# A product of two 4096 x 4096 matrices with GELU: the order of ScalarE, VectorE and both transfer queues made anew

## The chip, the cores and the metric

The kernel runs on one core of a Trainium2 chip. Its engines are TensorE (PE, matrix products), VectorE (DVE), ScalarE (ACT), GpSimd (POOL) and SyncE (SP); the last two are used here for little else than to start transfers (DMAs). Each engine works off its own list of instructions in a fixed order and waits, at each one, for the events that it needs. The metric is the time of one execution on the device, in microseconds (us); lower is better. A change of about 0.3% is what a measurement of this kernel tells from none.

## The reference

```python
def reference(a, b):                      # a, b: 4096 x 4096, float32
    x = np.matmul(a, b)
    return 0.5 * x * (1 + np.tanh(np.sqrt(2 / np.pi) * (x + 0.044715 * x**3)))
```

## The kernel before

The product is computed in half precision by a scheme of Strassen's kind, at two levels: a block of the output is made of seven products (P1 to P7) of sums and differences of quarter blocks instead of eight products, and a quarter is partly cut so once more. After 35 products that only warm TensorE and 32 plain ones come 6640 matmuls of 128 x 128 by 128 x 512 or 256. Their operands are such sums: VectorE forms them (helper `combine2`, line 964: 128x2048 or 128x4096 halves), after it has turned the blocks of `a` (line 656, transposes of 32 x 32). VectorE also adds finished products into the output sums (lines 1322 and 1327, from the accumulators), ScalarE copies accumulators (line 1981 to 1984), applies the GELU (line 1296) and squares the inputs for a running check of their size (line 1408, with VectorE's additions of line 1413).

The inputs `in_a_dram` and `in_b_dram` come in by POOL's queue, in pieces of 128 KB (b) and 256 KB (a). Sums that are used again are stored to a scratch unit in memory (`k_unit`, 512 KB) by SP's queue and fetched again by POOL's. Results go out by SP's queue (`out_dram`). All tiles lie in cells of a fixed set, named bR_73 to bR_80, aT, aD, stage_86, stage_87 (big ones) and y (small ones); a load into a cell must wait until the last user of what was there is done.

**What sets the order.** The kernel's body first only records operations. Each of the helpers `pe`, `dve`, `act` and `dma` (lines 824 to 838) calls `plan.add` with an estimated duration and the cells read and written, and the operation gets the next number, 0 to 4687. A planner (class `Plan`, line 323) then does three things: `schedule` (line 404) plays the engines forward by those durations, and picks for each engine the ready operation that is due first; `moved_order` (line 493) takes the planned order of each engine other than PE and applies the table `AFTER` to it, pair by pair; `emit` (line 504) plays the durations through once more in that fixed order and issues all operations in the order of their planned starts. TensorE's own order is that of recording. The heart of `moved_order` is

```python
for n, m in AFTER:
    o, row = self.ops[n], order[self.ops[n].eng]
    row.remove(o)
    row.insert(row.index(self.ops[m]) + 1 if m is not None else 0, o)
```

so a pair (n, m) puts operation n directly behind operation m on its engine. The planner's idea of a transfer is in three tables of numbers: `MOVE` is how long one takes by itself (us), `WEIGHT` its share when others are under way, and `UNDER_WAY` says what is under way when the plan begins. At most eight transfers of a queue are outstanding (`LANES = 8`). On the chip none of these numbers exists; there only the order on each engine is left, and the waits that the cells demand.

Of the kernel before, what the change touches and what calls it, by code (L numbers as in the profile page):

```python
# [52 lines left out]
UNDER_WAY = {"POOL": [(0.68, 12.2)] * 4}  # L53
# [7 lines left out]
    "store": 1.345, "fetch": 1.38, "quarter": 1.6, "piece": 1.27, "out": 0.73, "raw_a": 1.3, "raw_b": 0.645,  # L61
    "raw_a0": 1.363, "raw_b0": 0.64, "tiny": 0.2, "out_half": 0.3,
}
WEIGHT = {
    "raw_a0": 1.31, "raw_b0": 1.06, "store": 2.0, "fetch": 2.42, "quarter": 2.16, "piece": 2.16, "raw_a": 1.11,
    "raw_b": 1.06, "out": 1.05,
# [15 lines left out]
def modes_of(**kw):  # L82
# [2441 lines left out]
```

## Time and profile before

| | |
|---|---|
| median of three runs | 1445.19 us (1443.98 to 1448.59) |
| profiled execution, whole time | 1448.0 us |
| its span (first to last instruction) | 1446.4 us |
| granted TensorE clock, mean | 0.999 |
| PE busy | 1419.4 us, 98%, 6707 matmuls |
| DVE busy | 1238.0 us, 86% |
| ACT busy | 692.1 us, 48% |
| POOL busy | 487.5 us, 34% |
| moved by transfers | 380.99 MB, 263 GB/s in the mean |

Busy time is the time in which an engine executes something. In a row of a timeline the first number is the start from the span's begin, the second the length, then engine, line of the kernel, operation, written and read tiles (buffer numbers left out), shape, and after x the count of like instructions that follow each other; in brackets the idle time ahead of the row and what ended it. In a row of the waits: the engine and the matmul's line, what it waited for, the time in all, how often, the longest. A row of the windows gives, for a stretch of time, its length, then the busy time and count of PE, of its weight loads, of DVE, ACT and POOL, then TensorE's clock, the share of the transfer engines in use, and GB/s. A row of DMA issues ends with the size of one and the median time from issue to landing.

### The profile page before, as it was taken

The numbers are of one execution on the slowest core, as the hardware profiler recorded it, in microseconds if no ns is written. First come the engines' busy times: TensorE is split into PE (matmuls) and PEld (weight loads), VectorE is DVE, ScalarE is ACT, GpSimd is POOL, SyncE is SP. The second block draws the span as 40 slices with busy tenths as digits, with TensorE's granted clock in tenths as the row PEclk, the third lists the DMA queues.
The fourth block names the chain that finished last, engine by engine and source line by source line (L and its number), as shares of the span: only waits on it lengthen the run. The fifth ranks groups of instructions, "written<-read, shape, count | busy, mean of one in ns | idle before, by whom it ended". The sixth has DMA issues, their size and how long they took to land. (4 is left out here: it accounts for less than half of the span.)

```text
span 1446.4 us, 19351 instructions
## 1 busy us (share of the span) xinstructions
PE 1419.4 (98%) x6707; PEld 656.3 (45%) x6707; DVE 1238.0 (86%) x1331; ACT 692.1 (48%) x1492; POOL 487.5 (34%) x892
## 2 busy tenths in 40 slices
PE   8989999999999999999999999999999999999998
PEld 3434455465444444444444444444444444444443
DVE  2997797998889999979897988887998998878876
ACT  4966656358866313543655313353463622333133
POOL 6554245054225152324423342332322231231220
PEclk9999999999999999999999999999999999999999
DMA  9999999999999998989979897998998967796773
GB/s 171 203 241 272 311 298 266 338 237 271 295 299 248 335 201 231 310 276 276 321 259 318 274 216 270 257 248 276 280 348 241 302 160 228 273 313 217 260 256 140
DMA packets 207674, 380.99 MB, mean 263 GB/s; under 512 B 20944, under 2 KB 119760, under 8 KB 207568
## 3 DMA queue, kind: packets, MB, share of 16 engines
q0 software_dynamic: 150400, 247.52, 71.7%
q1 hardware_dynamic: 57168, 132.15, 24.4%
q8 instruction: 55, 0.90, 0.2%
q14 instruction: 51, 0.42, 0.1%
HBM read 339.74 MB, written 134.22 MB: 328 GB/s over the span
## 5 line engine op out<-in xcount | busy, mean ns | idle before, releaser
L1972 PE MATMUL acc<-bR 128*128 128x512 f16 x1568 | 346.8, 379 | 0.4 <-DVE bR L964 0.2
L1972 PEld LDWEIGHTS <-bR 128*128 128x128 f16 x1984 | 193.9, 98 | 235.0 <-DVE bR L964 1.3
L1972 PE MATMUL acc<-bR,aT 128*128 128x512 f16 x1280 | 283.4, 379 | 4.8 <-DVE bR L964 3.9
L1972 PEld LDWEIGHTS <-aT 128*128 128x128 f16 x1664 | 162.6, 98 | 202.0 <-issue 6.2
L838 POOL DMA_DIRECT2D bR<-k_unit x224 | 121.4, 545 | 367.9 <-PE acc L1972 265.2
L964 DVE TENSOR_TENSOR bR<-bR 128x4096 f16<-128x4096 f16 (+1 forms) x114 | 210.6, 1858 | 29.6 <-PE acc L1972 20.3
L838 POOL DMA_DIRECT2D bR<-in_b_dram x320 | 173.6, 546 | 159.0 <-DMA bR<-in_b_dram 61.3
L1984 ACT COPY acc<-acc 128x512 f32<-128x512 f32 x168 | 95.7, 574 | 274.7 <-PE acc L1972 247.4
L1322 DVE TENSOR_TENSOR y<-acc,y 128x512 f32<-128x512 f32 x269 | 177.1, 685 | 25.1 <-PE acc L1972 24.2
L1972 PE MATMUL acc<-bR,aD 128*128 128x512 f16 x736 | 163.6, 379 | 0.0
L1296 ACT ACTIVATE y<-y 128x512 f32<-128x512 f32 x174 | 105.3, 625 | 112.2 <-DVE y L1322 111.9
L1972 PEld LDWEIGHTS <-aD 128*128 128x128 f16 x1024 | 100.2, 98 | 120.8
L744 PE MATMUL acc<-bR,aT 128*128 128x512 f16 x544 | 119.9, 379 | 2.2 <-DVE y L1322 1.2
L744 PEld LDWEIGHTS <-aT 128*128 128x128 f16 x768 | 75.1, 98 | 92.3 <-issue 3.3
L1981 ACT COPY y<-acc 128x512 f32<-128x512 f32 x114 | 66.4, 585 | 94.5 <-PE acc L1972 87.1
L1408 ACT ACTIVATE y<-bR 128x1024 bf16<-128x1024 f16 x83 | 84.9, 1051 | 36.5 <-DVE y L1413 33.8
L838 POOL DMA_DIRECT2D stage<-in_b_dram x104 | 56.3, 546 | 121.9 <-PE acc L1045 32.3
L744 PEld LDWEIGHTS <-aD 128*128 128x128 f16 x608 | 59.4, 98 | 77.9 <-DVE aD L964 4.2
L1972 PE MATMUL acc<-stage,bR 128*128 128x512 f16 x416 | 94.0, 379 | 0.0
L1413 DVE TENSOR_TENSOR y<-y 128x1024 bf16<-128x1024 bf16 x102 | 70.0, 688 | 25.6 <-ACT y L1408 24.0
L1972 PE MATMUL acc<-stage,aT 128*128 128x512 f16 x384 | 86.8, 379 | 0.0
L1327 DVE TENSOR_TENSOR acc<-acc,y 128x512 f32<-128x512 f32 x115 | 78.9, 693 | 5.3 <-ACT y L1981 5.0
(128 smaller groups left out, 1769.0 us busy)
## 6 DMA issues: line engine op xcount, KB each, us to landing
bR<-k_unit POOLq DMA_DIRECT2D x224, 512.0 KB, 7.8
out_dram<-y SPq DMA_DIRECT2D x194, 256.0 KB, 6.8
bR<-in_b_dram POOLq DMA_DIRECT2D x328, 128.0 KB, 7.0
k_unit<-bR SPq DMA_DIRECT2D x78, 512.0 KB, 7.0
stage<-k_unit POOLq DMA_DIRECT2D x60, 512.0 KB, 7.0
bR<-in_a_dram POOLq DMA_DIRECT2D x64, 256.0 KB, 9.2
k_unit<-stage SPq DMA_DIRECT2D x30, 512.0 KB, 8.0
out_dram<-bR SPq DMA_DIRECT2D x56, 256.0 KB, 6.7
```

The lines of the kernel that those rows point to most:

```text
L744: nc.tensor.matmul(acc, sa[:, j // 2, i * P : (i + 1) * P, j % 2], sb[:, j, :], start=start and j == 0, stop=stop and j == 3, skip_group_c ...
L838: return plan.add(queue, COST[queue], lambda: eng.dma_start(out=dst, in_=src), r=r, w=w, size=MOVE[what] * SPREAD, weight=weight, **kw)
L964: nc.vector.tensor_tensor(out=dst, in0=xa, in1=ya, op=ALU.add if op > 0 else ALU.subtract)
L1296: act("gelu", lambda: nc.scalar.activation(t, t, ACT.Gelu_apprx_tanh), [("f", f)], [("f", f)])
L1322: dve("add", lambda: nc.vector.tensor_tensor(out=sm(g), in0=bank(s, i), in1=sm(f), op=ALU.add), [("f", f)], [("f", g), ("p", s, i)])
L1327: dve("add", lambda: nc.vector.tensor_tensor(out=bank(s, i), in0=bank(s, i), in1=sm(f), op=ALU.add), [("f", f)], [("p", s, i)])
L1408: act("square", lambda t=t, src=src: nc.scalar.activation(t, src, ACT.Square), [c(cx)], [("f", f)], slack=60.0, lead=lead)
L1413: dve("add16", lambda t=t, u=u: nc.vector.tensor_tensor(out=u, in0=u, in1=t, op=ALU.add), [("f", f)], [("f", e)], slack=60.0, lead=lead)
L1972: nc.tensor.matmul(bank(w, i), sa[:, jx // 2, r * P : (r + 1) * P, jx % 2], bv[:, jx, :], start=p in "17" and jx == 0, stop=jx == NJ - 1, ...
L1981: act("copy", lambda: nc.scalar.copy(out=sm(f), in_=bank(w, i)), [("p", w, i)], [("f", f)])
L1984: act("copy", lambda: nc.scalar.copy(out=bank(*dst), in_=bank(*x)), [("p", *x)], [("p", *dst)])
```

## The change

The three tables of the planner's durations get other numbers, and `AFTER` is a new table of 1580 pairs instead of 1131. Nothing else is edited: both programs record the same 4688 operations with the same needs, the same tiles and the same cells, and TensorE's instructions stand in the same order. Of the 1286 operations recorded for VectorE 356 keep their place in the order, of ScalarE's 1150 it is 318, of POOL's 872 transfers 175, of SP's 397 transfers 127. Most moves are short: half of them pass by less than about 1.2 us of the engine's own work. The new table has more lines, so line numbers behind it are 63 higher in the changed kernel (964 is 1027, 838 is 901).

```diff
-UNDER_WAY = {"POOL": [(0.68, 12.2)] * 4}
+UNDER_WAY = {"POOL": [(0.68, 13.2)] * 4}
...
 MOVE = {
-    "store": 1.345, "fetch": 1.38, "quarter": 1.6, "piece": 1.27, "out": 0.73, "raw_a": 1.3, "raw_b": 0.645,
-    "raw_a0": 1.363, "raw_b0": 0.64, "tiny": 0.2, "out_half": 0.3,
+    "store": 1.31, "fetch": 1.291, "quarter": 1.6, "piece": 1.27, "out": 0.743, "raw_a": 1.304, "raw_b": 0.649,
+    "raw_a0": 1.377, "raw_b0": 0.6444, "tiny": 0.2, "out_half": 0.3,
 }
 WEIGHT = {
-    "raw_a0": 1.31, "raw_b0": 1.06, "store": 2.0, "fetch": 2.42, "quarter": 2.16, "piece": 2.16, "raw_a": 1.11,
-    "raw_b": 1.06, "out": 1.05,
+    "raw_a0": 1.263, "raw_b0": 1.13, "store": 2.06, "fetch": 2.18, "quarter": 2.16, "piece": 2.16, "raw_a": 1.22,
+    "raw_b": 0.98, "out": 1.14,
 }
...
 AFTER = [
...
-    (3139, 3166), (3161, 3146), (3156, 3161), (3515, 3370), (3516, 3386), (3520, 3516), (3599, 3579),
+    (3058, 3037), (3094, 3086), (3034, 3094), (3139, 3119), (3161, 3146), (3166, 3161), (3214, 3156),
...
 ]
```

What that does to the engines' lists is shown at three places. In each pair of lists the first is the kernel before, the second the changed one; a row is line, operation, tiles and shape, and x how many of the same follow each other.

The first place is VectorE's list in the stretch from about 84 to 93 us (rows 58 to 67 of its list before, 50 to 60 now). The matmuls that start at 94.38 need the second aD_84<-aD_81,aT_66 of the first list.

```order
L964 TENSOR_TENSOR aD_84<-aD_81,aT_66 128x2048
L964 TENSOR_TENSOR bR_74<-bR_76,bR_74 128x2048
L964 TENSOR_TENSOR bR_80<-bR_76,aD_82 128x2048 x2
L1322 TENSOR_TENSOR aD_83<-acc_105,aD_83 128x512
L964 TENSOR_TENSOR aT_72<-aT_66,aT_72 128x2048
L1322 TENSOR_TENSOR aD_83<-acc_106,aD_83 128x512
L1322 TENSOR_TENSOR y_89<-acc_108,y_89 128x512
L964 TENSOR_TENSOR aT_72<-aT_66,aT_72 128x2048
L1413 TENSOR_TENSOR y_96<-y_96,bR_78 128x1024
L964 TENSOR_TENSOR aD_84<-aD_81,aT_66 128x2048
```

```order
L1476 TENSOR_TENSOR y_97<-y_97,y_102 128x1024
L1027 TENSOR_TENSOR aT_72<-aT_66,aT_72 128x2048
L1476 TENSOR_TENSOR y_96<-y_96,bR_78 128x1024
L1027 TENSOR_TENSOR aD_84<-aD_81,aT_66 128x2048
L1476 TENSOR_TENSOR y_96<-y_96,bR_78 128x1024
L1385 TENSOR_TENSOR y_98<-acc_107,y_98 128x512
L1476 TENSOR_TENSOR y_96<-y_96,y_102 128x1024
L1027 TENSOR_TENSOR aD_82<-bR_74,bR_80 128x2048
L1385 TENSOR_TENSOR y_100<-acc_109,y_100 128x512
L1385 TENSOR_TENSOR y_99<-acc_108,y_99 128x512
L1027 TENSOR_TENSOR aD_82<-bR_74,bR_80 128x2048
```

The aD_84 operation needed at 94.38 stands as the fourth row of the second list, behind one of the two aT_72, ahead of both aD_82; the other aD_84 stands three rows further down, and one of the two bR_80 and the second aT_72 come later still.

The second place is POOL's list from about 127 to 165 us: loads of b, 128 KB each, into the cells bR_74, bR_76, bR_77 and bR_78, eight pieces to a cell, in the order in which the stage operations of VectorE use the cells. The last row of each list is the end of this run of loads.

```order
L838 DMA bR_74<-in_b_dram 32x4x512 x5
L838 DMA bR_76<-in_b_dram 32x4x512 x7
L838 DMA bR_77<-in_b_dram 32x4x512 x4
L838 DMA bR_78<-in_b_dram 32x4x512
L838 DMA bR_77<-in_b_dram 32x4x512
L838 DMA bR_78<-in_b_dram 32x4x512 x2
L838 DMA bR_77<-in_b_dram 32x4x512 x3
L838 DMA bR_78<-in_b_dram 32x4x512 x5
```

```order
L901 DMA bR_76<-in_b_dram 32x4x512 x3
L901 DMA bR_77<-in_b_dram 32x4x512 x3
L901 DMA bR_76<-in_b_dram 32x4x512 x2
L901 DMA bR_77<-in_b_dram 32x4x512 x2
L901 DMA bR_76<-in_b_dram 32x4x512
L901 DMA bR_77<-in_b_dram 32x4x512
L901 DMA bR_76<-in_b_dram 32x4x512
L901 DMA bR_78<-in_b_dram 32x4x512
L901 DMA bR_77<-in_b_dram 32x4x512
L901 DMA bR_78<-in_b_dram 32x4x512
L901 DMA bR_77<-in_b_dram 32x4x512
L901 DMA bR_78<-in_b_dram 32x4x512 x4
```

Before, all of bR_76 stands ahead of bR_77; now six loads of bR_77 stand between those of bR_76, and two of bR_78 further up still, among bR_74, where the second list does not reach. The last load of bR_76 stands eight entries later than before, and the last of the whole run is a load of bR_78 in both.

The third place is POOL's list from about 841 to 860 us, the loads of b into stage_86, bR_74, bR_77 and stage_87. The sum that VectorE forms from stage_87 is needed by the matmuls of 863.99.

```order
L838 DMA stage_86<-in_b_dram 32x4x512
L838 DMA bR_77<-in_b_dram 32x4x512 x5
L838 DMA bR_74<-in_b_dram 32x4x512 x3
L838 DMA stage_87<-in_b_dram 32x4x512 x8
L838 DMA bR_77<-in_b_dram 32x4x512
L838 DMA bR_75<-k_unit_233 128x2048
L838 DMA bR_78<-k_unit_254 128x2048 x2
```

```order
L901 DMA stage_86<-in_b_dram 32x4x512
L901 DMA bR_77<-in_b_dram 32x4x512 x3
L901 DMA stage_86<-in_b_dram 32x4x512
L901 DMA bR_74<-in_b_dram 32x4x512
L901 DMA bR_77<-in_b_dram 32x4x512 x2
L901 DMA bR_74<-in_b_dram 32x4x512 x3
L901 DMA stage_87<-in_b_dram 32x4x512 x8
L901 DMA bR_78<-k_unit_254 128x2048 x2
```

The one load of bR_77 that stood behind the eight of stage_87 stands ahead of them now, and the fetch into bR_75 behind the two of bR_78.

369 rows, old and new, of the table AFTER are left out of this document.

## The prediction
> **What bounds the kernel now.** I read the page first, then TensorE's waits, then TensorE's timeline, and at each stall the timeline of the engine that ended it.
>
> ```profile
> span 1446.4 us, 19351 instructions
> PE 1419.4 (98%) x6707; PEld 656.3 (45%) x6707; DVE 1238.0 (86%) x1331; ACT 692.1 (48%) x1492; POOL 487.5 (34%) x892
> DMA  9999999999999998989979897998998967796773
> PE acc L1972 40%; DMA bR<-k_unit 1%; DVE bR L964 1%; DMA stage<-in_b_dram 0%; POOL stage L838 0%; DMA bR<-in_b_dram 0%; POOL bR L838 0%; DVE stage L964 0%; DVE bR L1322 0%; DVE acc L1327 0%; ACT y L2150 0%; DVE y L1322 0%; DVEq L964 0%; POOLq L838 0%
> ```
>
> The reader is to see that TensorE has work for 98% of the span, that the transfers are full for the first 40% of it, and that the chain's last 40% are matmuls without a gap. TensorE's order is the same in both programs, so its work of 1419 us is a floor, and the change can move only the waits. Three of them lie in the first 55 us, where the first loads come in (line, releaser, us in total, times, longest):
>
> ```profile
> PE acc L2260 <- DMA bR<-in_b_dram: 4.5, 3, 2.9
> PE acc L773 <- DVE aT L656: 1.6, 1, 1.6
> PE acc L753 <- DVE table L811: 1.5, 1, 1.5
> ```
>
> No order cures these 7.6 us. The others, by TensorE's timeline (in brackets the wait ahead of the row):
>
> ```profile
> 94.38 3.63 PE L744 MATMUL acc<-bR,aD 128*128 128x512 f16 x16 [1.87 <-DVE aD L964]
> 99.06 7.07 PE L744 MATMUL acc<-bR,aT 128*128 128x512 f16 x32 [1.05 <-ACT acc L2384]
> 107.46 7.08 PE L744 MATMUL acc<-bR,aD 128*128 128x512 f16 x32 [1.33 <-DVE aD L964]
> 115.70 7.07 PE L744 MATMUL acc<-aD,aT 128*128 128x512 f16 x32 [1.17 <-DVE aD L964]
> 171.41 7.07 PE L744 MATMUL acc<-stage,aD 128*128 128x512 f16 x32 [0.29 <-DVE stage L964]
> 180.32 7.07 PE L744 MATMUL acc<-stage,aD 128*128 128x512 f16 x32 [1.85 <-DVE stage L964]
> 283.90 3.61 PE L744 MATMUL acc<-bR,aT 128*128 128x512 f16 x16 [1.20 <-DVE y L1322]
> 448.55 3.61 PE L1972 MATMUL acc<-bR,aT 128*128 128x512 f16 x16 [1.48 <-DVE bR L964]
> 622.35 3.40 PE L1972 MATMUL acc<-bR,aT 128*128 128x512 f16 x15 [0.75 <-DMA bR<-in_b_dram]
> 716.57 2.75 PE L1972 MATMUL acc<-bR,aT 128*128 128x512 f16 x12 [0.17 <-DMA bR<-k_unit]
> 863.99 7.08 PE L1972 MATMUL acc<-bR,aT 128*128 128x512 f16 x32 [2.38 <-DVE bR L964]
> ```
>
> They sum to 13.5 us, 0.9% of the span: the most that an order could cure.
>
> **94 to 116 us: VectorE's work, and one set of loads.** VectorE runs back to back here:
>
> ```profile
> 105.04 2.36 DVE L964 TENSOR_TENSOR aD<-aT,aD 128x2048 f16<-128x2048 f16 x2
> 113.29 2.36 DVE L964 TENSOR_TENSOR aD<-bR 128x2048 f16<-128x2048 f16 x2 [2.42 <-DMA bR<-in_b_dram]
> 75.00:120.00 45.00, 39.58 (x181) 17.61 (x181) 42.20 (x54) 25.31 (x79) 23.18 (x43) 1.00 1.19 247
> ```
>
> The new order puts the aD operation that released the matmuls of 94.38 well ahead, so most of that wait of 1.87 goes (an operation of the same matmuls moves down, to about its old place); and the copy on ScalarE behind the 1.05 starts earlier. The pair at 105.04 (first row), which releases 107.46, has the very same operations ahead of it in both orders. VectorE is busy 42.20 us of the 45 (the third engine in the last row), so that pair ends where it ended, at best 0.5 earlier: what the first two waits give is taken back by a longer wait at 107. The set of eight loads behind 113.29 comes two entries earlier in POOL's queue, each entry a 0.54 us issue: -1.1 us at 115.70. In sum TensorE gets to the next part 0.5 + 1.1 = 1.6 us earlier at most, and 0 at least.
>
> **157 to 187 us: a queue that keeps its length.** Between 120 and 185 us POOL issues one 128 KB load whenever one lands. VectorE's timeline shows two sets' last loads, and POOL's the spacing:
>
> ```profile
> 170.13 2.36 DVE L964 TENSOR_TENSOR stage<-bR,stage 128x2048 f16<-128x2048 f16 x2 [1.78 <-DMA bR<-in_b_dram]
> 179.04 1.23 DVE L964 TENSOR_TENSOR stage<-bR,stage 128x2048 f16<-128x2048 f16 x1 [1.80 <-DMA bR<-in_b_dram]
> 162.63 1.22 DVE L964 TENSOR_TENSOR stage<-bR,stage 128x2048 f16<-128x2048 f16 x1
> 147.11 0.54 POOL L838 DMA_DIRECT2D bR<-in_b_dram  x1 [0.81 <-DMA bR<-in_b_dram]
> 156.50 4.44 POOL L838 DMA_DIRECT2D bR<-in_b_dram  x7 [0.37 <-DMA bR<-in_b_dram]
> bR<-in_b_dram POOLq DMA_DIRECT2D x328, 128.0 KB, 7.0
> 120.00:185.00 65.00, 62.86 (x291) 28.37 (x290) 49.58 (x64) 45.16 (x59) 20.65 (x39) 1.00 1.12 306
> ```
>
> Three sets of eight stand in this queue: bR_76 (for the stage operation of 162.63), bR_77 (170.13) and bR_78 (179.04). Now bR_78 and bR_77 have loads ahead of the last of bR_76, whose issue moves from 147.11 back by eight entries, to the second of the seven of 156.50, 157.2. With 7.0 us to landing (page, median) it lands at 164.2, and the operation ends 1.22 later at 165.4. The matmuls that wait for it began at 164.05 (171.41 less the wait of 0.29 and the 7.07 of a group of 32): a new wait of 1.4 us, or 0 if loads come in faster. The late end: the load that ended the wait at 170.13 is the fifth of those seven; eight entries took 157.2 - 147.11 = 10.1 us, 1.3 each, so three entries ahead of it is 166.2, plus 1.22, a wait of 3.4. But the last entry of the queue is a load of bR_78 as before, behind the same bytes on transfers that are full (1.12 in the last column but one), so 179.04 and with it 180.32 stay. The new wait and the 1.6 us gained up to here both end in the wait of 1.85 there. Net of both parts: **0**. The bounds: if the queue's last landing comes 1.85 earlier, the waits of 0.29 and 1.85 and the 1.6 us all count, -3.7; if bR_76 lands at the late end, TensorE comes 3.4 - 0.29 - 1.85 = 1.3 too late, +1.3.
>
> Here the Trainium skill, DMA: Bandwidth & Descriptors, Two DMAs through the same engine are not ordered, says that transfers start in order in a queue and may finish in another. By that, the +0.5 at 863.99 below could be 0 and the time 1444.2. The trace does not agree for these sets: the loads that end the waits at 170.13 and 179.04 are those issued last of their eight, so I keep the places.
>
> **283.90.** VectorE shows no idle ahead of either of the first two rows below. One operation of the pair aD<-aT,aD (1.22 us) goes behind the released one, and in their place come two y additions from further up.
>
> ```profile
> 282.03 1.22 DVE L964 TENSOR_TENSOR aD<-aT,aD 128x2048 f16<-128x2048 f16 x1
> 283.16 2.48 DVE L1322 TENSOR_TENSOR y<-acc,y 128x512 f32<-128x512 f32 x4
> 446.21 2.29 DVE L964 TENSOR_TENSOR bR<-bR 128x4096 f16<-128x4096 f16 x1 [1.66 <-DMA bR<-in_a_dram]
> ```
>
> By work alone the wait of 1.20 goes; by those additions, which wait for ScalarE, nothing does. I take the middle, **-0.6** (-1.2 to 0.2).
>
> **448.55** hangs on the transfer ahead of 446.21 (last row above), and the last of its loads has the same entry of the queue: **0** (-0.5 to +1.3, the spacing of one entry, since the set ahead has its last load one entry later).
>
> **622.35 and 716.57** wait for a load each that stands one entry earlier now: -0.75 and -0.17, **-0.9** (0 at the other end).
>
> **863.99.** POOL issues the eight loads of stage_87 here, and VectorE's sum waits for the last:
>
> ```profile
> 850.41 4.87 POOL L838 DMA_DIRECT2D stage<-in_b_dram  x8 [0.65 <-DMA bR<-in_b_dram]
> 855.38 0.54 POOL L838 DMA_DIRECT2D bR<-in_b_dram  x1
> ```
>
> The one load of bR_77 that stood behind them (855.38, 0.54 us) goes ahead: **+0.5** (0 to 1.1).
>
> **All else**, 866 to 1440 above all, has no wait now, and can only get one. Some fifteen operations move later by 0.5 to 5 us against a margin of 0.2 to 2 us. I price one wait of 283.90's size (1.20) at a bit under half its odds: **+0.5** (0 to 4).
>
> **Sum**: 0 - 0.6 + 0 - 0.9 + 0.5 + 0.5 = -0.5. The profiled execution took 1448.0 us (span 1446.4, 1.6 around it), 2.8 over the median of the runs shown, 1445.19; that 2.8 is no part of the change. Forecast: 1448.0 - 0.5 = 1447.5 on the profile's footing, **1444.7** on the median's.
>
> **Rival 1, faster: the first half's transfers come earlier.** The order rests on corrected durations, and it starts SP's second store of bR_73 directly behind its first; POOL waits for that cell here:
>
> ```profile
> 95.27 3.55 POOL L838 DMA_DIRECT2D bR<-in_b_dram  x6 [2.67 <-DMA stage<-in_b_dram]
> ```
>
> If this gap of 2.67 closes and the whole queue up to 180 us moves up with it, the -3.7 above counts. With 283.90 (-1.2) and -0.9, less 0.5: -5.3, so **1439.9**. For it: the gap is there. Against it: the transfers are already at 1.19 in that window, so bytes that start earlier push others later. The Trainium skill, Trainium Kernel Development and Optimization, Key Constraints, says the same of all queues, that they share 16 engines and interleave; by it this rival gives nothing and 1444.7 stands. Stores that fall behind loads can still shift some time, so I leave it **0.27**.
>
> **Rival 2, slower: a store goes late and its fetch stops POOL.** One of SP's two stores k_unit<-stage of 861.66 moves nine entries down, behind the first out store of 886.30; its fetch stays at POOL's 885.38.
>
> ```profile
> 861.66 0.87 SPq L838 DMA_DIRECT2D k_unit<-stage  x2
> 886.30 5.57 SPq L838 DMA_DIRECT2D out_dram<-y  x3
> 885.38 1.16 POOL L838 DMA_DIRECT2D stage<-k_unit  x2
> 912.35 3.62 PE L1972 MATMUL acc<-stage,aD 128*128 128x512 f16 x16
> k_unit<-stage SPq DMA_DIRECT2D x30, 512.0 KB, 8.0
> stage<-k_unit POOLq DMA_DIRECT2D x60, 512.0 KB, 7.0
> ```
>
> Store at 886.7, landed 8.0 later at 894.7; fetch then, landed 7.0 later at 901.7 (both medians): TensorE needs it at 912.35, so 10.6 us are left, and POOL is held from 885.4 to 894.7, 9.3 us. It decides once the held fetches, 512 KB each, queue up to more than those 10.6. Were half of the 9.3 to reach TensorE, with like ones for some later stores, it is +5.2 with the rest of my sum: **1450.4**. For it: nothing before 1440 us recovers a wait after 866, TensorE being without a gap. Against it: the margin is longer than the hold. **0.20**, with the other new waits in the unpriced rows.
>
> **How the numbers follow.** A change of 0.3% (4.3 us) is about what a measurement can tell from none: the three runs lie that far apart. My forecast, no measurable difference, has **0.53**, rival 1 **0.27**, rival 2 **0.20**. Its own range is 1441.5 to 1448.5 (below, the -3.7 against one more late wait of 0.5; above, the two bounds of 1.3 and one more wait of 1.2). To leave out two in ten I go to **1438.5** (rival 1 with the 1.48 of 448.55 too) and **1451** (just past rival 2). Faster 0.27, same 0.53, slower 0.20.
>
> **What would show it.** Right: in the new profile 180.32 stays within 1 us, a wait at about 164 is new, the waits at 94 and 99 are gone and that at 107 is longer; 622 and 717 have none; 864 has one of about 2.9. Rival 1 is shown by a set bR_78 that is complete before 177 us; rival 2 by TensorE waiting for stage<-k_unit after 900. I am wrong if waits after 866 sum to more than 4 us, or if the matmuls of 180.32 start over 3 us earlier.

## The result: 0.7% slower

The changed kernel takes 1455.60 us in the median of five runs (1452.75 to 1461.24), the kernel before 1444.87 us beside it (1443.98 to 1448.59): a ratio of 1.0072, 95% interval 1.0052 to 1.0092. The forecast was 1444.7 us with a range up to 1451; the result lies above it. The profiled execution of the changed kernel took 1452.75 us, the fastest of its five, and that of the kernel before 1448.0, near its slowest. So the two traces differ by 4.8 us and the medians by 10.7 us, and part of the work below is to say which differences between the traces are of the change.

The page of the changed kernel, its span, busy times and the chain that ended last:

```profile
span 1451.2 us, 19253 instructions
PE 1422.7 (98%) x6707; PEld 656.8 (45%) x6707; DVE 1235.9 (85%) x1331; ACT 685.2 (47%) x1492; POOL 487.8 (34%) x892
PE acc L2035 62%; PE acc L807 15%; DMA bR<-in_b_dram 5%; DMA stage<-in_a_dram 3%; DMA bR<-k_unit 3%; PE acc L1108 3%; DMA bR<-in_a_dram 2%; POOL bR L901 1%; DMA stage<-k_unit 1%; POOL stage L901 1%; DMA stage<-in_b_dram 1%; DVE stage L1027 1%; DVE bR L1027 0%; ACT y L1471 0%; DMA out_dram<-y 0%
```

TensorE has the same matmuls and 3.3 us more busy time. The half-rate clock told of below takes 3.9 us of it in the changed kernel and, at 23 us, 1.5 us in the kernel before. The 62% of the chain on matmuls lie in pieces with waits between them, the last at 1221.28, while the 40% before were one run of matmuls from 863.99 on: the late stalls have changed places. TensorE's timeline at the places that the prediction named, and at the new ones:

```profile
77.32 0.38 PE L807 MATMUL acc<-bR,aT 128*128 128x512 f16 x1 [1.67 <-DMA bR<-in_b_dram]
77.86 8.54 PE L807 MATMUL acc<-bR,aT 128*128 128x512 f16 x31 [0.16 <-DMA bR<-in_b_dram]
100.04 3.62 PE L807 MATMUL acc<-bR,aT 128*128 128x512 f16 x16
105.09 3.61 PE L807 MATMUL acc<-bR,aT 128*128 128x512 f16 x16 [1.43 <-ACT acc L2447]
109.78 7.08 PE L807 MATMUL acc<-bR,aD 128*128 128x512 f16 x32 [1.08 <-DVE aD L1027]
116.69 7.07 PE L807 MATMUL acc<-aD,aT 128*128 128x512 f16 x32
172.46 19.89 PE L807 MATMUL acc<-stage,aD 128*128 128x512 f16 x81 [7.26 <-DVE stage L1027]
290.75 3.62 PE L807 MATMUL acc<-bR,aT 128*128 128x512 f16 x16
455.31 3.61 PE L2035 MATMUL acc<-bR,aT 128*128 128x512 f16 x16 [1.02 <-DVE bR L1027]
867.01 7.07 PE L2035 MATMUL acc<-bR,aT 128*128 128x512 f16 x32
968.45 3.40 PE L2035 MATMUL acc<-bR,aD 128*128 128x512 f16 x15 [0.91 <-DMA bR<-in_b_dram]
1221.28 3.63 PE L2035 MATMUL acc<-bR 128*128 128x512 f16 x16 [0.31 <-DVE bR L1027]
```

Read each start against that of the same matmuls before. The lag is 100.04 - 99.06 = 1.0 us, at the next part of the program still 116.69 - 115.70 = 1.0; then 172.46 - 164.05 = 8.4; 290.75 - 283.90 = 6.9; 455.31 - 448.55 = 6.8; 867.01 - 863.99 = 3.0; and 4.8 at the end of the span. In this pair of traces one wait of 7.26 us, at the matmuls of the stage operand, is the largest loss, and the stall at 863.99, now gone, gives some 3 us back. The other 6 of the 10.7 us between the medians lie in executions that left no trace.

The wait of 7.26, by VectorE's timeline of the changed kernel:

```profile
169.44 1.23 DVE L1027 TENSOR_TENSOR stage<-bR,stage 128x2048 f16<-128x2048 f16 x1 [9.29 <-DMA bR<-in_b_dram]
171.19 1.22 DVE L1027 TENSOR_TENSOR stage<-bR,stage 128x2048 f16<-128x2048 f16 x1
```

It is the set bR_76 that comes late, as the prediction had it, but at 169.2 and not at 164.2: its last load, the row below, was issued at 158.54 (forecast 157.2) and took 10.6 us to land (forecast 7.0).

```profile
158.54 0.54 POOL L901 DMA_DIRECT2D bR<-in_b_dram  x1 [0.96 <-DMA bR<-in_b_dram]
```

Behind the landing stand three operations and not one. VectorE forms the stage operand in two halves, and each needs the whole set bR_76. The half that TensorE's first matmuls need stands second in both lists, behind the other half and the additions between. In the kernel before it is the prediction's row at 162.63; the other half is this one:

```profile
159.07 1.22 DVE L964 TENSOR_TENSOR stage<-bR,stage 128x2048 f16<-128x2048 f16 x1
```

In the changed kernel the landing is at 169.17, the halves are formed at 169.44 and 171.19 with one addition between them, and TensorE starts at 172.46, 3.3 us behind the landing where the prediction had 1.22.

What lies beside the load is in SP's list. SP's timeline before, where the long gap ahead of 156.50 is a wait of the queue at one out store, and then after:

```profile
144.71 0.44 SPq L838 DMA_DIRECT2D k_unit<-stage  x1
156.50 0.33 SPq L838 DMA_DIRECT2D out_dram<-y  x1
156.88 0.93 SPq L838 DMA_DIRECT2D k_unit<-aD  x2
157.91 1.36 SPq L838 DMA_DIRECT2D k_unit<-stage  x1
```

```profile
144.21 0.33 SPq L901 DMA_DIRECT2D k_unit<-aD  x1
147.00 1.64 SPq L901 DMA_DIRECT2D k_unit<-stage  x2
157.72 2.26 SPq L901 DMA_DIRECT2D out_dram<-y  x2
```

One store of aD and one of a stage cell, 512 KB each, have moved from behind that out store to ahead of it. Between the issue and the landing of the last bR_76 load six stores land in the changed kernel, 2.25 MB. The moved store of the stage cell is one of them; that of aD is not, it lands at 156.4.

Last, the windows around both new stalls, after and then before (the clock is the last column but two):

```profile
75.00:85.00 10.00, 8.17 (x31) 3.16 (x29) 9.95 (x13) 6.95 (x12) 7.30 (x13) 0.83 1.23 185
165.00:175.00 10.00, 2.74 (x8) 0.87 (x7) 5.12 (x7) 5.42 (x7) 2.16 (x4) 0.76 1.05 245
175.00:185.00 10.00, 10.00 (x43) 4.32 (x42) 9.90 (x11) 4.72 (x6) 0.00 (x0) 0.90 0.77 301
```

```profile
75.00:85.00 10.00, 10.00 (x47) 4.60 (x47) 9.72 (x14) 9.69 (x22) 4.90 (x9) 1.00 1.32 199
165.00:175.00 10.00, 9.71 (x46) 4.32 (x45) 7.44 (x9) 3.38 (x4) 0.54 (x1) 1.00 1.12 308
```

Behind each of the two new waits the granted clock is below 1: for eight to ten matmuls TensorE starts one in 0.43 us instead of 0.216. It costs 1.7 us at 77 us and 2.25 at 172 us, and no sentence of the prediction had a price for it. The kernel before shows one, behind a wait of 2.88 us: 25 matmuls take 7.09 us there and not 5.56, which is 1.5 us.

```profile
23.20 7.09 PE L2260 MATMUL acc<-bR,aT 128*128 128x512 f16 x25 [2.88 <-DMA bR<-in_b_dram]
```

### The profile page after: what moved, and what is told of

It reads as the page before. It is cut to its first block, busy times and chain, and to the rows that moved or that the text cites. A ratio compares the mean times of both kernels' runs of the same rounds, so it can differ in the third digit from the quotient of the medians.

```text
span 1451.2 us, 19253 instructions
## 1 busy us (share of the span) xinstructions
PE 1422.7 (98%) x6707; PEld 656.8 (45%) x6707; DVE 1235.9 (85%) x1331; ACT 685.2 (47%) x1492; POOL 487.8 (34%) x892
## 4 chain that ended last, share of the span: by engine, by line
PE 79%; DMA 14%; POOL 2%; DVE 2%; issue 2%; ACT 1%; DVEq 0%; POOLq 0%; ACTq 0%
PE acc L2035 62%; PE acc L807 15%; DMA bR<-in_b_dram 5%; DMA stage<-in_a_dram 3%; DMA bR<-k_unit 3%; PE acc L1108 3%; DMA bR<-in_a_dram 2%; POOL bR L901 1%; DMA stage<-k_unit 1%; POOL stage L901 1%; DMA stage<-in_b_dram 1%; DVE stage L1027 1%; DVE bR L1027 0%; ACT y L1471 0%; DMA out_dram<-y 0%
## 5 line engine op out<-in xcount | busy, mean ns | idle before, releaser
L2035 PE MATMUL acc<-bR,aD 128*128 128x512 f16 x736 | 163.8, 379 | 0.9 <-DMA bR<-in_b_dram 0.9
L807 PEld LDWEIGHTS <-aD 128*128 128x128 f16 x608 | 59.8, 99 | 82.3 <-issue 10.6
```

What stands on the lines that cost most here:

```text
L807: nc.tensor.matmul(acc, sa[:, j // 2, i * P : (i + 1) * P, j % 2], sb[:, j, :], start=start and j == 0, stop=stop and j == 3, skip_group_c ...
L2035: nc.tensor.matmul(bank(w, i), sa[:, jx // 2, r * P : (r + 1) * P, jx % 2], bv[:, jx, :], start=p in "17" and jx == 0, stop=jx == NJ - 1, ...
```

## The experiments

All of them give an engine a list that is put together from the kernel before and the changed kernel; no work differs. In the diffs `b` is the order before and `c` the changed one, of the four engines VectorE, ScalarE, POOL and SP. A cut at a time stands for the nearest place of the program at which both orders have issued the same entries: at 120 us these are the first 103, 145, 111 and 12 entries of the four engines, at 188 us 164, 207, 148 and 51. The kernel gets each list by a table `AFTER` that is made anew for it. Some of these kernels hold the old planner's numbers and some the changed; the list of each engine is the one told either way. Ratios are to the kernel before, run beside it.

**Which half.** The first two kernels cut the program at 188 us.

```diff
-order = c
+order = b[:188 us] + c[188 us:]      # e1_early_before
+order = c[:188 us] + b[188 us:]      # e2_late_before
```

> All four engines in the order of the kernel before up to about 188 us, in the changed order from there on. In the changed kernel TensorE is 8.2 us behind the kernel before at 188 us and 5.0 behind at the end. Theory A (the changed order is better behind 188 us: it removed the waits at 284, 622 and 864): those 3.2 us come without the early loss, 1444.9 - 3.2 = about 1441.7. Theory B (TensorE only came later, and so found done what it had waited for; the order behind 188 us gives nothing): the old waits are back and only the new ones at 964, 1213 and 1216 (1.1 + 0.5 + 0.5) are added, about 1445 to 1447.

> The other half: changed order up to about 188 us, order of before from there on. Theory A: the early loss of 8.2 us stays and nothing is won back, 1444.9 + 8.2 = about 1453. Theory B: the lateness is won back at the old waits (1.2 + 1.5 + 0.75 + 2.4 = 5.8 at most), 1444.9 + 8.2 - 5 = about 1448.

With the changed order late: 1.0015 (0.9998 to 1.0032). With the changed order early: 1.0097 (1.0080 to 1.0115), with the same wait. That is 12 us by the medians, more than the 8.2 that either theory started from. TensorE's timeline of e2:

```profile
170.30 21.89 PE L753 MATMUL acc<-stage,aD 128*128 128x512 f16 x89 [6.92 <-DVE stage L973]
870.61 8.75 PE L1981 MATMUL acc<-bR,aT 128*128 128x512 f16 x32 [3.11 <-DVE bR L973]
```

The loss is made in the first 188 us. All that the trace shows as gained behind that is not to be seen in the medians: of the late part alone no gain is measured, and its interval leaves room for 0.02% at most.

**The first 80 us, and the loads of 120 to 170 us.** In the second of these, POOL's entries 111 to 147 (37 loads) stand as before.

```diff
 order = c
+order = b[:80 us] + c[80 us:]                                  # e3_first80_before
+order["POOL"] = c[:111] + b[111:148] + c[148:]                 # e4_pool_loads_before
```

> The changed order, but with the order of before on all four engines up to about 80 us, where the changed kernel has new waits (1.7 us at 77 and a slower clock for 1.7 us behind it). Theory C (the loads of 120 to 170 us decide, in the order in which they stand): the wait at 172 stays within 2 us of 7.3, total within 2 us of the changed kernel, 1453.6 to 1455.6. Theory D (these loads are late because all of the queue starts 2.3 us later at 88 us): the wait at 172 shrinks by 2.3 or more and the total by 3 or more, 1452.5 or less.

> The changed order, but POOL's 37 loads of about 120 to 170 us in the order of before; all else as changed. Theory C: the wait of 7.3 us at 172 goes but for 1 to 2 us, and with it the slower clock behind it (2.1 us); TensorE is 1 to 3 us behind the kernel before at 188 us instead of 8.2, total 1447 to 1450. Theory D: the set of loads still comes late, the wait stays above 4 us, total above 1452.

e3: 1.0091 (1.0064 to 1.0118), no gain. The mixture makes a wait of its own, and the old one stays, by TensorE's timeline of e3:

```profile
122.01 8.61 PE L807 MATMUL acc<-aD,aT 128*128 128x512 f16 x32 [6.98 <-DVE aD L1027]
177.61 14.55 PE L807 MATMUL acc<-stage,aD 128*128 128x512 f16 x54 [5.55 <-DVE stage L1027]
```

So e3 says nothing of the first 80 us by itself, beyond that the wait at the stage operand doesn't need them. e4: 1.0037 (1.0023 to 1.0050); the wait at 164 to 172 is gone, and one of 2.42 stands at 174.20 in its place. The order of those loads is needed for the wait of 7 us. The whole time lies 5.8 us above the kernel before, more than the 2 to 5 us of theory C.

**The loads alone, and pieces of the late part.**

```diff
 order = b
+order["POOL"] = b[:111] + c[111:148] + b[148:]                 # e6_only_pool_loads
+order = b[:188 us] + c[188:905 us] + b[905 us:]                # e5_middle_after
+order = b[:736 us] + c[736:905 us] + b[905 us:]                # e8_736_to_905
```

> The kernel before with one thing of the change: POOL's 37 loads of about 120 to 170 us in the changed order. If that order makes the wait at 172 by itself (theory C): a wait of 4 to 8 us where TensorE starts on the stage operand of bR_76, a slower clock for 2 us behind it, 5 to 8 us slower in all (0.35 to 0.55%). If it needs the later start of the queue or the other engines' new order too: under 3 us.

> Order of before up to about 188 us and again from about 905 us on, the changed order only between. In the profiled run of the kernel with the changed order all the way behind 188 us, TensorE gained 5.2 us on the kernel before between 188 and 865 us and lost 1.5 behind (waits at 964 and 1216). Theory A (the changed order is better between): 3 to 5 us faster than before, 0.2 to 0.35%, and at 864 no wait. Theory B (that profiled run was a lucky one; its ten times had the median of the kernel before): within 1 us of before.

> The kernel before with the changed order only between about 736 and 905 us. The forecast had +0.5 us at 864 here, the changed kernel showed -2.6. If the order of this stretch takes the wait at 864 away by itself (POOL's fetches ahead of the loads leave its eight places earlier): no wait at 864, a new one of 0.5 at 788, 2 to 3 us faster. If the wait went for what came before 736 us: the wait of 2.4 us stays, no change.

e6: 1.0030 (1.0011 to 1.0050), and a wait inside the bounds that the prediction gave this term (1.4, at most 3.4). TensorE's timeline of e6, then VectorE's:

```profile
166.06 22.43 PE L745 MATMUL acc<-stage,aD 128*128 128x512 f16 x96 [2.93 <-DVE stage L965]
```

```profile
161.23 1.23 DVE L965 TENSOR_TENSOR stage<-bR,stage 128x2048 f16<-128x2048 f16 x1 [4.11 <-issue]
164.79 1.22 DVE L965 TENSOR_TENSOR stage<-bR,stage 128x2048 f16<-128x2048 f16 x1
```

The last bR_76 load is issued at 154.69 and lands 6.3 us later, at 161.0; one store, 0.25 MB, lands in that time. That is 3.2 us sooner than the forecast landing of 164.2, and the wait is still twice the 1.4: VectorE's old list has three additions between the two halves, and 5.1 us go from the landing to TensorE's start. So the number lay inside its bounds by luck, by two errors that cancel. From e6 to the changed kernel the landing is 8.2 us later, VectorE is 1.8 us shorter behind it, and TensorE itself comes 2.1 us later; that makes the 4.3 us between the two waits. e5 gives 1.0003 (0.9990 to 1.0016), so the waits that vanish between 188 and 905 us in the trace show no gain in the median. e8 gives 0.9983 (0.9968 to 0.9998), the only kernel of this study below 1: 1445.02 us in the median. That is below the 0.3% that a measurement tells from none, and the lowest of fifteen kernels. The wait at 864 is gone in it, by POOL's timeline and then TensorE's:

```profile
847.04 4.80 POOL L847 DMA_DIRECT2D stage<-in_b_dram  x8 [0.42 <-PE acc L1981]
```

```profile
860.24 7.07 PE L1981 MATMUL acc<-bR,aT 128*128 128x512 f16 x32
```

POOL issues the eight loads of stage_87 here 860.24 - 847.04 = 13.2 us ahead of the matmuls that need their sum. Before, it was 863.99 - 850.41 = 13.6 us with the wait of 2.38 in it, so 11.2 without. They come 2 us earlier in the program, and that is the wait. It is not the place of the one bR_77 load behind them, on which I had put the price: 0.54 us can't make 2.

**What makes the landing 8 us later.** I took first POOL's stop ahead of two early loads of bR_78, then SP's list.

```diff
 order = c
+order["POOL"]: the two early loads of bR_78 behind the last of bR_76    # e7_two_loads_back
+order["SP"] = b[:51] + c[51:]                                          # e9_stores_before
+order["SP"] = b[:51] + c[51:]; order["POOL"] = c[:111] + b[111:148] + c[148:]   # e12_both_before
```

> The changed kernel with two loads of bR_78 (the first of that set, ahead of the last loads of bR_74) put behind the last load of bR_76. Two things follow: POOL no longer stops at 133 to 137.6 us for the cell of bR_78, which ScalarE frees (4.35 us of waiting there), and the last load of bR_76 stands two entries earlier (1.3 us each). Theory E (the stop at the head of the queue counts): the wait of 7.3 us at 172 shrinks by 4 to 5 us. Theory C alone (only the entries count): by 2.6 us. Total 3 to 6 us faster than the changed kernel.

> The changed kernel with SP's first 51 stores (up to about 188 us) in the order of before. Theory F (the wait of 7.3 us at 172 is the eight entries of POOL's queue plus about 1 MB of stores that SP now issues at 144 to 148 us instead of 157 us, so that they compete with the last loads of bR_76): the wait shrinks from 7 to about 3 us, as in the run with POOL's loads alone, and the wait of 1.8 us at 75 goes too (SP's second store of bR_73 is issued at 83 instead of 55 us); 5 to 8 us faster than the changed kernel, 1447 to 1451. Theory G (the loss comes from VectorE's and ScalarE's order and from the later start of the queue): the wait at 172 stays above 5.5 us.

> The changed kernel with both taken back: SP's first 51 stores and POOL's 37 loads of 120 to 170 us in the order of before. Theory F: no wait above 1.5 us between 160 and 185 us, TensorE there within 2 us of the kernel before, total within 0.2% of before (1443 to 1449). Theory G: more than 0.3% slower than before stays.

e7: 1.0045 (1.0028 to 1.0062), and the wait is 6.88 at 170.89, nearly the same: a miss. The last bR_76 load is issued 3.7 us earlier, at 154.79, and takes 13.0 us to land instead of 10.6, with 2.75 MB of stores beside it. So an earlier place in POOL's queue alone gains little there. e9: 1.0022 (1.0004 to 1.0040). With SP's stores as before, and the loads in the changed order, both new waits are gone, at 77 and at 172 us; the last bR_76 load is issued at 154.56 and lands 6.0 us later with 0.5 MB of stores beside it. What is left is a wait that this mixture makes, at 143 us, where ScalarE waits for a store of a cell that it will overwrite. It makes TensorE 4.2 us later; without it TensorE would have come to the stage operand about 2.9 us too early (an estimate: 165.1 less 4.2, against 163.8, when VectorE has formed the half that it needs). So the landing is what e9 shows, 8.6 us sooner, and not that the whole wait goes with the stores. ScalarE's timeline of e9, then TensorE's:

```profile
141.51 1.06 ACT L1471 ACTIVATE y<-stage 128x1024 bf16<-128x1024 f16 x1 [7.45 <-DMA out_dram<-y]
```

```profile
143.59 1.02 PE L807 MATMUL acc<-bR,aT 128*128 128x512 f16 x4 [3.25 <-ACT acc L1575]
```

e12 gives 1.0027 (1.0009 to 1.0044), with no wait between 160 and 185 us and one of 4.66 at 145.42 of the same kind. So SP's order is what the late landing needs beside the loads' order. It does not say how much of the order before can be kept without a new wait.

**One store, and loads with stores, put into the kernel before.**

```diff
 order = b
+order["SP"] = c[:4] + b[4:]                                            # e10_one_store_early
+order["POOL"] = b[:111] + c[111:148] + b[148:]; order["SP"] = b[:13] + c[13:51] + b[51:]   # e11_loads_and_stores
```

> The kernel before with one store moved: SP's store of bR_73's second half first instead of fourth, so at about 55 instead of 83.6 us. If it is this 0.5 MB that makes the loads of 60 to 75 us late: a wait of about 1.8 us at 75 us and a slower clock behind it, TensorE 2 to 4 us later at 80 us; of which most is taken back by shorter waits up to 116 us. If not, TensorE is where it is before at 80 us, within 0.5 us. Total within 2 us of before in both cases.

> The kernel before with POOL's 37 loads of about 120 to 170 us and SP's stores 14 to 51 (about 121 to 188 us) in the changed order, nothing else. POOL's loads alone gave a wait of 2.9 us at 166. Theory F: with the stores it is 6 to 8 us, with 2 us of slower clock behind it, 6 to 9 us slower than before in all. Theory G: 2 to 4 us as with the loads alone.

e10: 1.0000 (0.9983 to 1.0016). The store of 54 us gives a wait of 1.19 at 75.70, where runs with the order before up to there have 0.41 at most, and no half-rate clock; the median doesn't show it. So the store alone is not the price of the first 80 us. e11: 1.0043 (1.0027 to 1.0058); the last bR_76 load is issued at 155.59 and lands 9.3 us later, at 164.9, with 2.0 MB of stores beside it: between the 161.0 of the loads alone and the 169.2 of the changed kernel. TensorE itself was late there by a wait of 3.15 at 117.98, again one of the mixture, so its own wait was only 1.83, less than either theory had.

**Cut where nothing is mixed.** The last three kernels avoid such mixtures by cutting all four engines at 120 us.

```diff
 order = b
+order = b[:120 us] + c[120:188 us] + b[188 us:]                        # e13_120_to_188
+order = c[:120 us] + b[120 us:]                                        # e14_first_120
+order = c[:120 us] + b[120:736 us] + c[736:905 us] + b[905 us:]; order["SP"][:4] = b[:4]   # e15_best
```

> The kernel before, with the changed order on all four engines only between about 120 us and 188 us of the program; the order before stands ahead of that and behind it. If this stretch by itself makes the loss (SP's two stores to k_unit and POOL's loads both in it): a wait of TensorE of at least 5 us between 160 and 175 us, with the half-rate clock of about 2 us behind it, and 0.4 to 0.7% slower than before. If the loss needs what the changed first 120 us do to SP and POOL as well: a wait of about 3 us there, as with the 37 loads alone, and at most 0.35% slower.

> The kernel before, with the changed order on all four engines only up to about 120 us; the order before stands behind that. If the first 120 us hold the rest of the loss: the wait of 1.8 us at 75 us and 1.7 us of half-rate clock behind it, 0.2 to 0.4% slower than before. If the waits that go between 94 and 116 us take that back: within 0.15% of before, with TensorE's lag at 116 us near 1 us and no new wait between 160 and 175 us.

> A candidate: the changed order up to about 120 us, but SP's first four stores as before, then the order before up to 736 us, the changed order from 736 to 905 us, and the order before behind. If the waits at 94, 99 and 116 us (some 2 us net) and the one at 864 us (2.5 us) are both worth their length: 0.2 to 0.35% faster than before, and faster than the 736 to 905 us stretch alone (0.9983). If the early waits are made up for later on before's own order: no better than that stretch alone.

e13, the stretch alone: 1.0019 (1.0003 to 1.0036). e14, the first 120 us alone: 1.0040 (1.0021 to 1.0059). TensorE's timeline of e13 and then of e14:

```profile
165.85 20.88 PE L748 MATMUL acc<-stage,aD 128*128 128x512 f16 x96 [2.66 <-DVE stage L968]
```

```profile
76.41 0.38 PE L746 MATMUL acc<-bR,aT 128*128 128x512 f16 x1 [1.66 <-DMA bR<-in_b_dram]
76.98 8.54 PE L746 MATMUL acc<-bR,aT 128*128 128x512 f16 x31 [0.20 <-DMA bR<-in_b_dram]
866.41 8.43 PE L1974 MATMUL acc<-bR,aT 128*128 128x512 f16 x32 [3.76 <-DVE bR L966]
```

In e14's trace TensorE is 3.4 us behind the kernel before at 81 us, level with it at 118 us (0.1) and at 188 us (-0.1), and 3.8 us behind at the end; 2.7 of these arise at 866.41, where the order is that of before. So where the 0.40% of the first 120 us arise is not shown.

The stretch from 120 to 188 us, with the same loads and stores in the same order as in the changed kernel, waits 2.66 and not 7.26. The wait of 7 us needs both parts. The waits of SP's queue from 120 to 135 us show what the first part hands on, in the changed kernel and then in e13:

```profile
SPq L901 <- DMA stage<-in_b_dram: 5.1, 1, 5.1
```

```profile
SPq L842 <- DMA stage<-in_b_dram: 1.7, 1, 1.7
```

Ahead of the stores in question stands one, `k_unit<-stage`, that waits for the last load of a stage cell. That load lands at 129.5 in the changed kernel and at 124.5 in e13. Of the stores behind it eight go 5 to 6 us later, the store of aD at 144.21 where it went at 138.46 in e13; the store of a stage cell that was moved ahead lands at 159.7 where it landed at 153.6. In e13 these stores are through when the last bR_76 load is issued, at 156.41: 0.25 MB land beside it, and it takes 6.1 us. In the changed kernel the two stores of stage cells issued at 147 to 148 us stand beside it, with those behind them: 2.25 MB and 10.6 us. That fits e9 too, where the moved stores stay behind the out store and the load lands, at 160.6, before the first of them (162.6). This chain is read from the two traces; no run moves that one load of the stage cell alone. Of the 6.6 us from 162.6 (e13) to 169.2, 4.5 are the longer transfer and 2.1 the later issue. In numbers of the last landing: before 156.9; the 37 loads alone 161.0; loads and stores of the stretch 162.6; with the first 120 us 169.2.

By medians the two parts alone are worth 0.19% and 0.40%, 0.59% in sum, and both together 0.97% (e2): the rest, 0.38% or 5.5 us, is what they do to each other. The three intervals together leave about 0.3% either way, so this rest is only just clear of zero. The two waits differ by 4.6 us, and the half-rate clock of 2.25 stands behind the long one alone: 6.9 us, which agrees within that margin.

e15 gives 1.0001 (0.9988 to 1.0015), 1447.32 us: no better than e8. It has two waits at 141 to 144 us that neither kernel has (0.78 and 1.31, for ScalarE's copy), which take back most of the early gains; whether these would last without them stays open. No version here beats the kernel before by more than e8's 0.17%.

## Why the prediction was wrong, point by point

The step that failed is the term of 157 to 187 us, which the prediction put at 0: a late set bR_76 whose wait would vanish in the wait of 180.32. It cost 7.2 us between the two traces.

The terms of the sum, in us, against the change of TensorE's lag between the two profiled executions (starts of the same matmuls; a row takes in all that lies between the row above and its place):

| place | forecast | measured |
|---|---|---|
| up to 90 us | 0 (not spoken of) | +4.2 |
| 94 to 116 | -1.6 to 0 | -3.2 |
| 157 to 187 | 0 with the part above | +7.2 |
| 283.90 | -0.6 | -1.4 |
| 448.55 | 0 | -0.1 |
| 622.35 and 716.57 | -0.9 | -0.7 |
| 863.99 | +0.5 | -3.0 |
| all else | +0.5 | +2.0 |
| sum | -0.5 | +5.0 |

**157 to 187 us is the term that decided it.** That bR_76 would come late, and that a wait of the stage matmuls would be new, was right. The size, 1.4 with an end at 3.4, was counted from places in POOL's queue alone. From start to start the wait is 7.4 us. Of the 6.0 beyond the forecast, the landing gives 5.0 (1.3 by the later issue, 3.6 by the longer transfer) and the other half of the stage operand and the addition, which VectorE does first, 2.1; TensorE itself came 1.0 later, which takes off 1.0. For the loads alone the size looked right (2.93 in e6, 2.66 in e13), but these sets landed 3.2 and 1.6 us sooner than forecast, and VectorE's part, 5.1 and 3.3 us for 1.22, made up for it. I left out SP's list, though the same diff reorders it. The 7.0 us to landing was the page's median over the whole run; the very load that set the place took 9.8 before (147.11 to 156.9, with 1.75 MB of stores beside it), and what it takes at its new place hangs on which stores are beside it then: 6.3 in e6, 10.6 in the changed kernel.

**"The last entry of the queue is as before, so 180.32 stays" was false.** The last load landed at 174.5 and not at 178.7. No store lands beside it, between 168.9 and 175.7, since SP's next one holds a stage cell and can go only at 172.44, when VectorE has formed the late second half (it ends at 172.41):

```profile
172.44 0.33 SPq L901 DMA_DIRECT2D k_unit<-stage  x1
```

The waits at 171.41 and 180.32 are gone and give 2.5 us, against 7.4 lost and 2.25 of half-rate clock. The step "the new wait and the 1.6 gained both end in the wait of 1.85" compared waits at two places as if only their sum mattered; a wait longer than the later slack passes through it.

**Up to 90 us was left out.** I read SP's early store of bR_73 as rival 1's advantage. In the changed kernel the loads of 60 to 75 us are late, and TensorE waits 1.83 us at 77 for one of them, with 1.7 us of half-rate clock behind it. e14 shows the same two numbers. The store alone (e10) gives 1.19 and no measurable time, so it is one cause among others of the first 80 us; the rest is open.

**94 to 116 us** gave more than its bounds: the waits of 94.38, 99.06 and 115.70 are gone, and the one at 107.46 became shorter (1.08), where the forecast had it longer and taking the gain back. ScalarE's copy is a new one at 105.09 (1.43), which I had not seen. Part of it is that TensorE came 4.2 us late: where it came on time (e9, e12, e15) the stretch gave 2.2 to 2.3 us. And in six other runs with the order before it the stretch itself lies between 0.1 later and 1.3 sooner than in the profile of before. But e14, which has them all, is slower, and e15 is not faster: no kernel showed these 3 us as a gain of time.

**283.90, 622.35, 863.99** vanished, 716.57 stayed (0.23), and the forecast for 863.99 had the wrong sign. More than that, I took one execution's waits for the kernel's. With the order before in force at 864, the trace of each run shows a wait there of 2.38 (the kernel before), 2.31 (e10), 1.28 (e13), 0.97 (e11), 0.31 (e6), 3.11 (e2) and 3.76 us (e14). At 283.90 the wait is there, 0.48 to 1.51 us, in five other runs in which TensorE comes no later than in the kernel before, and missing in three in which it comes 1 to 6 us later. So a trace that gets 3.0 us at 863.99 shows no gain (e5) to 0.17% (e8) in the medians. By the times alone: 4.8 us between the traces, and 3.1 by which the one lies above its median, and 2.9 by which the other lies below, make the 10.7. The sentence "that 2.8 is no part of the change" was true of the footing and false of the waits counted on it.

**All else**: new waits at 968.45 and 1221.28 and small ones beside them, 2.0 for a forecast of 0.5, inside its bounds (0 to 4).

**The rivals.** Rival 1 needed bR_78 complete before 177 us, and it was, at 174.5, with no gain: that sign could not tell the rival from a queue whose bytes had changed places. Rival 2's late store made no wait: there is none for stage<-k_unit after 900 us. Its side was right and its mechanism wrong. What I named as a sign of error, waits after 866 of over 4 us, did not come (2.0); the loss stood where I had written 0.

## What to carry to other kernels

When a change reorders several queues that share full transfer engines, count the bytes of all of them that land beside a critical load, and not its place in its own queue alone; here 2 MB of stores of another queue made a load's 6 us into 10 or 11. Before a stall of a profile is entered as a gain, ask whether other executions have it: at 863.99 the wait was 0.3 to 3.8 us in runs with one and the same order there. Count all operations that stand in the list between a landing and the engine that waits, and ask which of them could stand behind: here the half needed later was formed first. And price a wait of TensorE with what follows it, here 1.4 to 2.7 us where half-rate clock came.

## What the runs showed of the hardware

**The half-rate clock behind a wait depends on more than its length.** The rows of e2 at the first new wait are these; it is the wait of the changed kernel at 77.32, of the same length, with the same matmuls behind it:

```profile
76.24 0.38 PE L753 MATMUL acc<-bR,aT 128*128 128x512 f16 x1 [1.67 <-DMA bR<-in_b_dram]
76.77 6.85 PE L753 MATMUL acc<-bR,aT 128*128 128x512 f16 x31 [0.16 <-DMA bR<-in_b_dram]
```

The 31 matmuls take 6.85 us here and 8.54 in the changed kernel. Of five runs with this wait (1.66 to 1.67 us) three have slow matmuls behind it (the changed kernel, e4, e14) and two have none (e2, e7). The wait of 2.66 in e13 has no slow matmuls behind it (20.88 us for 96), nor the one of 3.25 in e9 (the four matmuls behind it take 1.02); the one of 2.93 in e6 has (22.43 for 96). The Trainium skill, TensorE: Matmul & The Clock Gate, What's actually happening, speaks of half rate after about 3.4 us of idleness in a window that runs freely; the traces agree with the half rate (0.43 against 0.216 us from start to start) and not with the length: the gap in the changed kernel, 1.67 and 0.16, is about half of that. What decides between two waits of the same length no run here shows.

**A 128 KB load takes longer, the more bytes of the other queue land beside it.** In every run of this study seven other loads land between the issue and the landing of the last bR_76 load, wherever it stands. What differs is the stores of SP's queue that land in that time:

| run | stores landing beside it | issue to landing |
|---|---|---|
| e6, e13 | 0.25 MB | 6.3, 6.1 us |
| e9, e3 | 0.5 MB | 6.0, 8.1 us |
| e1, e10 | 1.25 MB | 8.2, 8.3 us |
| e8 | 1.5 MB | 8.6 us |
| before, e2, e5, e15 | 1.75 MB | 9.8, 9.1, 9.3, 11.0 us |
| e11, e14 | 2.0 MB | 9.3, 10.9 us |
| the changed kernel | 2.25 MB | 10.6 us |
| e12, e4 | 2.5 MB | 11.3, 13.8 us |
| e7 | 2.75 MB | 13.0 us |

That is some 2 to 3 us for each MB of stores: (10.6 - 6.1) / 2.0 = 2.25 between e13 and the changed kernel, (13.0 - 6.3) / 2.5 = 2.7 between e6 and e7. A load that takes longer has also more time for stores to land in, so the slope is not all cause. Stores that were under way when the load was issued are free of that: with 0.25 or 0.5 MB of them (e3, e6, e9, e13) the load took 6.0 to 8.1 us, with 1.0 to 1.5 MB (the changed kernel, e1, e2, e8, e10, e15) 8.2 to 11.0, and with 1.75 to 2.5 MB (the kernel before, e4, e5, e7, e11, e12, e14) 9.3 to 13.8. The ranges overlap, so the stores are not all that decides.
